# A two-layer transformer block: the second layer's weights split into high and low parts during the first layer and kept in device memory

## The chip, the core and the metric

The kernel runs on one core of a Trainium2 chip. The metric is the device time of one execution in microseconds. TensorE multiplies matrices, VectorE and ScalarE work on rows of 128 partitions, GpSimd (POOL in the rows) does the same more slowly, and SyncE issues the transfers; its queue is called SP in the rows.

## What is computed

A backbone of two layers on 512 latent tokens and 256 context tokens of width 1024. Each layer has a mixing part and a feed-forward part. In short:

```
for l in range(2):
    h  = modulate(rms_norm(x), shift, scale)
    pa, q, k, v, pc = split(h @ w_in[l])       # 2560 columns: A 512, Q 512, K 512, V 512, C 512
    ya = u * (w_s @ layer_norm(v_a))           # group A: gelu, gate mixed over 128 positions
    yb = rms_norm(softmax(q1 k1) v - lam * softmax(q2 k2) v)   # group B: 4 heads, rotary positions
    yc = silu(layer_norm(dwconv31(a * sigmoid(g))))            # group C
    x  = x + gate * (concat(ya, yb, yc) @ w_out[l])
    h2 = modulate(rms_norm(x), ...)
    x  = x + gate2 * ((silu(dwconv3(h2 @ w_gate)) * (h2 @ w_val)) @ w_down)
```

Context tokens go through the same weights. In the second layer only their K and V are needed. The output is the latent stream.

## The kernel before

All matrix products are made three times: every operand is split into a high part (rounded to the type that TensorE takes at full speed, fp32r) and a low part (the rest), and high x high, high x low and low x high are added up in PSUM. So each weight must be split before its use. `wsplit` does that: it loads a tile (512 KB, tag `raw`, three buffers) on the sync queue, makes the high part by a ScalarE copy (line 220) and the low part by a subtraction (line 106) on VectorE or GpSimd, in tiles of tags `hi` and `lo` with two buffers each. Copy and subtraction have a raised priority. Which of the two engines subtracts is written out by hand: `WE` has one letter for each of 20 chunks of w_in and each layer, d for VectorE and p for GpSimd; the calls for w_out, w_gv (gate and value) and w_down name the engine.

One layer runs in stages. In the projection stage, `proj_tok` multiplies the tokens by one block of 512 columns of w_in at a time, in four chunks of 256 rows (`k2`), six or four PSUM tiles of 128 tokens in parallel. For each chunk it first does all products with the high part of the weight (lines 389 and 390), then those with the low part (line 397). The order of the blocks in the second layer is: K for the two context tiles, C (lines 441 to 443), A, K for the four latent tiles, Q, V. Between the products, at fixed steps (`AH`, `KH`, `CH`), hooks put in the small matrix work of the other groups: the gate of A (`pg`), the flips of K into its transposed form (`pk`, line 577), the sums of C's norm (`cm`, `cv`). The depthwise convolution of group C is 60 multiply-adds on VectorE (line 647) with lowered priority, which fill VectorE's gaps; `c_finish` needs all of them. `qk_tile` makes the norm and the rotation of a tile of Q or K on VectorE and ScalarE with two tables GC and GS, which GpSimd makes from ropet and gbase.

Then come the attention stage (scores, softmax, products with V, with a part of the output projection filled in between) and the rest of the output projection (`wout_w`, `wout`). The feed-forward part runs in two halves of 11 blocks of 128 columns: `gv` for each block, then four pairs of output rows (`mp2`) with w_down. In the second half of the first layer the last pair (`tail`) is done first for the context and then for the latent tokens, so that the next layer's norm can begin.

The order on each engine is made when the program is built: a scheduler takes the instructions by priority, which is the order of the code moved by `high_priority` and `low`, and the engines then keep that order. A transfer in the sync queue whose buffer is not yet free therefore holds up all transfers behind it.

## Time and profile before

| | us |
|---|---|
| median of 3 runs (1637.74 to 1638.4) | 1638.32 |
| profiled execution | 1637.72 |
| its span on the chip | 1635.9 |

Busy time in the span: TensorE 1574.7, VectorE 1033.9, ScalarE 646.2, GpSimd 178.3 us. 162.08 MB are moved, at 99 GB/s over the span.

A row of a table of stages gives a stretch, its length, the busy time of each engine in it with the number of instructions, the granted clock of TensorE as a share of full speed, the share of the 16 DMA engines and their GB/s. Groups are instructions with the same line, engine, operation and shape. A busy TensorE need not be at its peak, since products overlap: one product of 512 columns is recorded with some 0.4 us, though the next one starts 0.23 us after it.

### The profile page before, as it was taken

The page shows a single profiled execution, that of the slowest core. Times are in us where ns is not written, and L with a number is a line of the kernel's source. Part 1 is how long each engine was busy: PE and PEld are TensorE (multiplying, and loading weights), DVE is VectorE, ACT ScalarE, POOL GpSimd, SP SyncE. Part 2 cuts the span into 40 slices and gives each one's busy share as a digit, 9 for nine tenths or more (in the row PEclk, how much of TensorE's full clock was granted, in tenths as well). Part 3 has the DMA queues.
Part 4 walks back from the last instruction along what each step waited for, and adds up shares of the span by engine and source line. Part 5 has one row for each costly group of instructions (what it writes and reads, how often), then busy time and mean ns, then how long its engine had stood idle before and what let it go on. Part 6 is the DMA issues. An engine that isn't in the chain of part 4 may idle for free.

```text
span 1635.9 us, 20796 instructions
## 1 busy us (share of the span) xinstructions
PE 1574.7 (96%) x8186; PEld 1294.7 (79%) x8186; DVE 1033.9 (63%) x1666; ACT 646.2 (40%) x1098; POOL 178.3 (11%) x158
## 2 busy tenths in 40 slices
PE   7999998999999999999999999779999999999999
PEld 5865776778888888888888878567778788888888
DVE  4597878969999862244333277996987544244433
ACT  5431568753523221133232244255775433123321
POOL 1130224310000000000000023341420000000000
PEclk8999999999999999999999999889999999999999
DMA  8625110014355852111122223221001223332232
GB/s 286 201 96 171 42 62 14 14 64 169 104 193 194 290 192 70 66 65 62 56 65 58 84 87 110 62 65 52 27 27 65 91 90 96 88 101 97 96 100 94
DMA packets 57409, 162.08 MB, mean 99 GB/s; under 512 B 9056, under 2 KB 11360, under 8 KB 57184
## 3 DMA queue, kind: packets, MB, share of 16 engines
q1 hardware_dynamic: 57312, 160.76, 30.3%
q8 instruction: 64, 1.05, 0.3%
q14 instruction: 33, 0.27, 0.0%
HBM read 158.64 MB, written 2.10 MB: 98 GB/s over the span
## 4 chain that ended last, share of the span: by engine, by line
PE 83%; DVE 10%; ACT 4%; issue 1%; DMA 1%; POOL 0%; POOLq 0%; DVEq 0%; SPq 0%; ACTq 0%
PE pp L227 13%; PE pp L226 13%; PE pp L228 13%; PE pd L228 6%; PE pd L226 6%; PE pd L227 6%; PE acc L389 4%; PE acc L390 4%; PE acc L397 3%; DVE cacc L647 3%; PE po L816 2%; PE mr L156 2%; PE wo L226 1%; PE wo L227 1%; PE wo L228 1%
## 5 line engine op out<-in xcount | busy, mean ns | idle before, releaser
L220 ACT CAST whi<-raw 128x1024 fp32r<-128x1024 f32 (+2 forms) x199 | 204.3, 1029 | 550.9 <-PE pp L227 251.0
L106 DVE TENSOR_TENSOR wlo<-raw,whi 128x1024 fp32r<-128x1024 f32 (+1 forms) x163 | 196.9, 1210 | 304.9 <-ACT whi L220 297.4
L227 PE MATMUL pp<-hlo,whi 128*128 128x512 f32 (+1 forms) x1072 | 380.7, 356 | 0.8 <-DVE hlo L266 0.8
L226 PE MATMUL pp<-hhi,whi 128*128 128x512 f32 (+1 forms) x1072 | 379.8, 356 | 1.5 <-ACT whi L220 1.3
L228 PE MATMUL pp<-hhi,wlo 128*128 128x512 f32 (+1 forms) x1072 | 378.9, 354 | 0.0
L226 PEld LDWEIGHTS pp<-hhi,whi 128*128 128x128 f32 x1072 | 201.4, 188 | 35.1 <-ACT whi L220 2.7
L227 PEld LDWEIGHTS pp<-hlo,whi 128*128 128x128 f32 x1072 | 201.5, 188 | 33.0 <-DVE hlo L266 1.5
L228 PEld LDWEIGHTS pp<-hhi,wlo 128*128 128x128 f32 x1072 | 201.5, 188 | 31.0
L106 POOL TENSOR_TENSOR wlo<-raw,whi 128x1024 fp32r<-128x1024 f32 (+1 forms) x36 | 100.3, 2788 | 870.3 <-ACT whi L220 716.9
L228 PE MATMUL pd<-gh,wlo 128*128 128x512 f32 (+1 forms) x550 | 192.4, 350 | 0.6 <-DVE wlo L106 0.6
L226 PE MATMUL pd<-gh,whi 128*128 128x512 f32 (+1 forms) x550 | 192.9, 351 | 0.0
L227 PE MATMUL pd<-gl,whi 128*128 128x512 f32 (+1 forms) x550 | 192.3, 350 | 0.0
L389 PE MATMUL acc<-whi,hhi 128*128 128x512 f32 x352 | 144.8, 411 | 2.8 <-ACT whi L220 2.8
L390 PE MATMUL acc<-whi,hlo 128*128 128x512 f32 x352 | 144.2, 410 | 0.0
L647 DVE SCALAR_TENSOR_TENSOR cacc<-cin,cw,cacc 128x783 f32<-128x783 f32 (+1 forms) x120 | 125.8, 1102 | 2.8 <-ACT cacc L642 2.7
L228 PEld LDWEIGHTS pd<-gh,wlo 128*128 128x128 f32 x550 | 103.4, 188 | 15.9 <-DVE wlo L106 0.8
L227 PEld LDWEIGHTS pd<-gl,whi 128*128 128x128 f32 x550 | 103.5, 188 | 15.1
L226 PEld LDWEIGHTS pd<-gh,whi 128*128 128x128 f32 x550 | 103.4, 188 | 14.9
L983 DVE TENSOR_TENSOR ft<-ft,pp 128x256 f32<-128x256 f32 (+1 forms) x66 | 39.4, 598 | 96.2 <-PE pp L228 84.7
L397 PE MATMUL acc<-wlo,hhi 128*128 128x512 f32 x352 | 94.0, 401 | 0.0
L389 PEld LDWEIGHTS acc<-whi,hhi 128*128 128x128 f32 x352 | 68.0, 193 | 25.0 <-issue 7.1
L192 DVE CUSTOM_DVE_ANT_0 mraw<-mraw,csil,bmod 128x1024 f32<-128x1024 f32 x64 | 81.7, 1280 | 8.0 <-DMA mraw<-in_w_modT_dram 7.8
(198 smaller groups left out, 2334.3 us busy)
## 6 DMA issues: line engine op xcount, KB each, us to landing
raw<-in_w_gv_dram SPq DMA_DIRECT2D x88, 512.0 KB, 3.2
mraw<-in_w_modT_dram SPq DMA_DIRECT2D x64, 512.0 KB, 4.2
raw<-in_w_in_dram SPq DMA_DIRECT2D x44, 512.0 KB, 3.6
raw<-in_w_down_dram SPq DMA_DIRECT2D x34, 512.0 KB, 3.6
mraw<-in_w_modN_dram SPq DMA_DIRECT2D x16, 512.0 KB, 5.9
mraw<-in_w_modH_dram SPq DMA_DIRECT2D x16, 512.0 KB, 3.9
raw<-in_w_out_dram SPq DMA_DIRECT2D x16, 512.0 KB, 3.2
raw<-in_w_down_dram SPq DMA_DIRECT2D x16, 384.0 KB, 3.2
```

Source lines behind the costliest of these rows:

```text
L106: (eng or V).tensor_sub(o, a, hi.bitcast(F32))
L156: T.matmul(o[r:r + 32], cs[:, k], w, start=k < 4, stop=k >= 4, tile_position=(0, r))
L192: r = V.tensor_tensor_reduce(out=junk, in0=w, in1=csil[:, s], scale=1.0, scalar=bmod[:, l, i, f:f + 1], op0=ALU.mult, op1=ALU.add, accum_o ...
L220: S.copy(hi, raw)
L226: T.matmul(o, lhi, rhi, start=start, stop=False)
L227: T.matmul(o, lhi, rlo, start=False, stop=False)
L228: T.matmul(o, llo, rhi, start=False, stop=stop)
L389: T.matmul(pt[t], hhi[hs], wh[:, a], start=k2 + a == 0, stop=False)
L390: T.matmul(pt[t], hlo[hs], wh[:, a], start=False, stop=False)
L397: T.matmul(pt[t], hhi[hs], wl[:, a], start=False, stop=k2 + 1 == KD // 2 and a == 1)
L647: V.scalar_tensor_tensor(out=cacc[:, c, :cn], in0=cin[:, c, j:j + cn], scalar=cw[:, l, c, j:j + 1], in1=cacc[:, c, :cn], op0=ALU.mult, op1 ...
L983: V.tensor_mul(t[:, a:b], t[:, a:b], pp[s][1][:, :b - a])
```

## The change

The second layer's w_in and w_out are split in the second half of the first layer's feed-forward part (`split_ahead`): 56 pieces of 128x512, each loaded, copied to the high part on ScalarE, subtracted on VectorE, and both parts stored to tiles in device memory. All transfers go by the sync queue. The pieces come at a lowered priority (`ALOW`): up to 3 after each of the 11 blocks of columns and up to 8 after each pair of output rows (`AHEAD`) until there are none left. In the second layer `wsplit_of` loads the two parts (512 KB each) instead of splitting; w_in's odd chunks use two of the three `raw` tiles, the even ones `hi` and `lo`. Two smaller edits concern both layers: GC and GS are made on VectorE, and the low part of w_s is subtracted on VectorE.

```diff
-WE = ("dpdpdpdddppdpppppddp", "pdpppppppppppppddpdd")
+WE = "dpdpdpdddppdpppppddp"
+AHEAD = (3, 8)
+ALOW = 60
...
+    dram = ctx.enter_context(tc.tile_pool(name="split", bufs=1, space=bass.MemoryType.DRAM))
+    split = {}
+
+    def w_cols(l, col, k2):
+        return w_in[l, 2 * k2 * P:(2 * k2 + 2) * P, col:col + 512].rearrange("(a p) n -> p a n", p=P)
+
+    def split_ahead(sp):
+        todo = [(("in", col, k2), [w_cols(1, col, k2)[:, a] for a in range(2)])
+                for col in (COL_K, COL_C, COL_A, COL_Q, COL_V) for k2 in range(KD // 2)]
+        todo += [(("out", q, mp2), [w_out[1, q, mp2, :, i].rearrange("p k m -> p (k m)") for i in range(2)])
+                 for mp2 in range(KD // 2) for q in range(2)]
+        for key, srcs in todo:
+            split[key] = dram.tile([P, 2, 2, 512], F32, name="_".join(map(str, key)))
+            for a, src in enumerate(srcs):
+                raw = sp.tile([P, 512], F32, tag="araw", name="araw", bufs=3)
+                hi = sp.tile([P, 512], F32R, tag="ahi", name="ahi", bufs=3)
+                nc.sync.dma_start(out=raw, in_=src)
+                S.copy(hi, raw)
+                sub_lo(raw, raw, hi)
+                nc.sync.dma_start(out=split[key][:, 0, a], in_=hi.bitcast(F32))
+                nc.sync.dma_start(out=split[key][:, 1, a], in_=raw)
+                yield
+
+    def wsplit_of(key, src, shape, eng, tags=("hi", "lo"), p=None, **kw):
+        if key not in split:
+            return wsplit(src, shape, eng, p=p, **kw)
+        r = []
+        for x, t in enumerate(tags):
+            w = (p or wp).tile([P] + shape, F32R, tag=t, name="w" + "hl"[x], bufs=RAWB if t == "raw" else 2)
+            flat = w.rearrange("p a n -> p a n") if len(shape) == 2 else w.rearrange("p a k m -> p a (k m)")
+            nc.sync.dma_start(out=flat.bitcast(F32), in_=split[key][:, x])
+            r.append(w)
+        return r
...
+            def wchunk(col, k2, **kw):
+                tags = ("raw", "raw") if k2 % 2 else ("hi", "lo")
+                return wsplit_of(("in", col, k2), wsrc(col, k2), [2, 512], wengine(col, k2), tags, **kw)
...
-                    wh, wl = wsplit(wsrc(col, k2), [2, 512], wengine(col, k2))
+                    wh, wl = wchunk(col, k2)
...
-                wh, wl = wsplit(wsrc(COL_C, k2), [2, 512], wengine(COL_C, k2), raw=pre.get(k2))
+                wh, wl = wchunk(COL_C, k2, raw=pre.get(k2))
...
-            wsh, wsl = wsplit(w_sT[l], [HEADS, P], p=sp, **(dict(bufs=1) if l else dict(tags=("mraw", "mraw"), bufs=MRB)))
+            wsh, wsl = wsplit(w_sT[l], [HEADS, P], "dve", p=sp, **(dict(bufs=1) if l else dict(tags=("mraw", "mraw"), bufs=MRB)))
...
-                G.tensor_mul(GC[:, j], ropet[:, 0], gbase[:, j, 0].unsqueeze(1).to_broadcast([P, NLT, QKD]))
-                G.tensor_mul(GS[:, j], ropet[:, 1], gbase[:, j, 1].unsqueeze(1).to_broadcast([P, NLT, QKD]))
+                V.tensor_mul(GC[:, j], ropet[:, 0], gbase[:, j, 0].unsqueeze(1).to_broadcast([P, NLT, QKD]))
+                V.tensor_mul(GS[:, j], ropet[:, 1], gbase[:, j, 1].unsqueeze(1).to_broadcast([P, NLT, QKD]))
...
-            return [(wsplit(w_out[l, q, mp2], [2, 4, P], eng, **kw), (yACh, yACl) if q == 0 else (yBh, yBl))
+            return [(wsplit_of(("out", q, mp2), w_out[l, q, mp2], [2, 4, P], eng, **kw), (yACh, yACl) if q == 0 else (yBh, yBl))
...
+                    if not last and half:
+                        with low(ALOW):
+                            for _ in zip(range(AHEAD[0]), ahead):
+                                pass
...
+                        if not last and half:
+                            with low(ALOW):
+                                for _ in zip(range(AHEAD[1]), ahead):
+                                    pass
...
+                    ahead = split_ahead(wt)
```

## Rows read from the trace of the kernel before

**Rows 1.** The page's busy time: us, share of the span, instructions.

```profile
PE 1574.7 (96%) x8186; PEld 1294.7 (79%) x8186; DVE 1033.9 (63%) x1666; ACT 646.2 (40%) x1098; POOL 178.3 (11%) x158
```

**Rows 2.** Table of stages: stretch, length, busy us (instructions), clock, DMA share, GB/s.

```profile
500.00:600.00 100.00, 100.00 (x568) 87.00 (x567) 91.51 (x160) 28.19 (x34) 0.00 (x0) 1.00 0.76 251
690.00:880.00 190.00, 190.00 (x1079) 165.29 (x1078) 75.33 (x100) 56.15 (x67) 0.00 (x0) 1.00 0.20 64
880.00:945.00 65.00, 65.00 (x374) 56.72 (x373) 20.32 (x29) 14.85 (x21) 2.39 (x1) 1.00 0.26 76
...
1003.50:1107.20 103.70, 81.92 (x363) 64.95 (x361) 99.74 (x142) 44.96 (x81) 38.91 (x17) 0.90 0.25 77
...
1143.50:1232.00 88.50, 82.80 (x433) 66.83 (x431) 75.73 (x139) 66.69 (x152) 30.99 (x45) 1.00 0.07 25
```

**Rows 3.** What TensorE waited for, 940 to 1290 us: total us, times, longest.

```profile
PE pk L577 <- DVE ks L106: 10.9, 3, 4.5
PE pg L226 <- ACT vbh L496: 8.7, 1, 8.7
```

**Rows 4.** Groups by shape, 940 to 1260 us: busy us, mean ns, idle before.

```profile
L647 DVE SCALAR_TENSOR_TENSOR cacc<-cin,cw,cacc 128x512 f32<-128x512 f32 x60 | 62.6, 1095 | 0.8 <-ACT cacc L642 0.8
L106 POOL TENSOR_TENSOR wlo<-raw,whi 128x1024 fp32r<-128x1024 f32 x22 | 57.0, 2590 | 713.1 <-ACT whi L220 643.3 <-PE acc L397 29.7 <-issue 15.3
```

**Rows 5.** The chain that ended last: start us, us, what.

```profile
968.25 0.24 PE acc L389
...
1048.08 0.66 DVE cacc L647
...
1089.09 0.43 PE acc L390
...
1140.61 2.80 PE acc L397 x12
```

**Rows 6.** Order of time, VectorE and GpSimd: start us, us, instructions.

```profile
1007.38 28.34 DVE L647 SCALAR_TENSOR_TENSOR cacc<-cin,cw,cacc 128x512 f32<-128x512 f32 x28 [0.80 <-ACT cacc L642]
...
1073.97 0.16 DVE L557 TENSOR_TENSOR nw<-nw,rk 128x8 f32<-128x8 f32 x1
...
1075.13 3.37 POOL L106 TENSOR_TENSOR wlo<-raw,whi 128x1024 fp32r<-128x1024 f32 x1 [4.66 <-ACT whi L220]
...
1076.15 2.37 DVE L557 TENSOR_TENSOR nw<-nw,rk 128x8 f32<-128x8 f32 x1
```

**Rows 7.** Groups by shape, 940 to 1260 us: a cast and a subtraction of 128x512.

```profile
L106 DVE TENSOR_TENSOR ks<-kx,ks 128x512 fp32r<-128x512 f32 x6 | 4.1, 681 | 1.4 <-ACT ks L595 1.4
...
L595 ACT CAST ks<-kx 128x512 fp32r<-128x512 f32 x6 | 3.7, 620 | 4.8 <-DVE kx L591 4.8
```

**Rows 8.** Transfers: KB each, median us to landing; and GB/s from 410 to 610 us.

```profile
GB/s 3 0 0 113 205 193 124 210 184 215 204 135 210 206 165 196 202 181 170 250 110 210 216 211 288 270 323 310 274 310 324 243 274 243 302 270 217 213 105 79
...
mraw<-in_w_modT_dram SPq DMA_DIRECT2D x53, 512.0 KB, 4.1
...
raw<-in_w_in_dram SPq DMA_DIRECT2D x13, 512.0 KB, 3.6
ropet<-in_rope_dram SPq DMA_DIRECT2D x1, 256.0 KB, 2.6
...
out_dram<-xT SPq DMA_DIRECT2D x4, 256.0 KB, 2.3
```

**Rows 9.** Groups by shape: GC on GpSimd, a product of that size on VectorE.

```profile
L543 POOL TENSOR_TENSOR GC<-ropet,gbase 128x256 f32<-128x256 f32 x2 | 2.4, 1194 | 0.2 <-DVE gbase L541 0.2
...
L565 DVE TENSOR_TENSOR qsq<-kx,GS 128x256 f32<-128x256 f32 x8 | 3.3, 416 | 0.0
```

**Rows 10.** What the sync queue waited for, 960 to 1260 us: total, times, longest.

```profile
SPq L212 <- POOL wlo L106: 134.9, 20, 15.7
...
SPq L536 <- DVE yA L505: 12.3, 1, 12.3
```

More of the change, by code (lines that the diff above doesn't have):

```diff
@@ L314, in wengine @@
             def wengine(col, k2):
-                return {"d": "dve", "p": "pool"}[WE[l][(col - COL_A) // 512 * 4 + k2]]
+                return {"d": "dve", "p": "pool"}[WE[(col - COL_A) // 512 * 4 + k2]]
             def wsrc(col, k2):
-                return w_in[l, 2 * k2 * P:(2 * k2 + 2) * P, col:col + 512].rearrange("(a p) n -> p a n", p=P)
+                return w_cols(l, col, k2)
+            def wchunk(col, k2, **kw):
+                tags = ("raw", "raw") if k2 % 2 else ("hi", "lo")
+                return wsplit_of(("in", col, k2), wsrc(col, k2), [2, 512], wengine(col, k2), tags, **kw)
             if l == 0:
```

## The prediction

> **What bounds the kernel now.** I read the table of stages first, then what TensorE waited for, then the groups of instructions by shape, then the order of time around the longest waits. TensorE is busy for 96% of the span [rows 1], so a change can win only where it is not. The stages [rows 2] show where that is: in the first layer's feed-forward part (500 to 600, 690 to 945 us) it is busy without a gap. In the second layer's projections, 1003.5 to 1107.2 us, it is busy for 81.92 of 103.70 us, at a granted clock of 0.90, while VectorE is busy for 99.74 us. The two long waits of TensorE there are for VectorE's work: 10.9 us on the flips of K (pk) and 8.7 us on group A's gate (pg) [rows 3]. So this stage is VectorE's.
>
> Why is VectorE full there? Its largest group is the depthwise convolution, 60 instructions of 1095 ns [rows 4]. The same instruction takes 0.66 us alone [rows 5], and 28 of them in a row took 28.34 us [rows 6], 1.01 each. What is beside the long ones is GpSimd's subtraction of a weight's low part: 22 of 2590 ns [rows 4]. The plainest case is an operation on 8 columns: 0.16 us alone, 2.37 us when GpSimd's 3.37 us subtraction of 1075.13 us runs [rows 6]. VectorE stands still while GpSimd subtracts. The convolution alone lost 60 x (1.095 - 0.66) = 26 us by it.
>
> **Part 1, the second layer's splits vanish.** Its 24 chunks of w_in and 8 of w_out need no ScalarE cast and no subtraction; 19 + 3 of these subtractions are GpSimd's, those above. First I ask how much TensorE time there is to win. From 968.25 us (its first product for the second layer) to 1143.41 us (the end of V's last) [rows 5] it has 48 + 96 + 96 + 96 + 96 + 144 = 576 products of 512 columns (K of the context, C, A, K, Q, V) at 2.80/12 = 0.233 us [rows 5], 134.4 us; with the flips, the gate and the norms' sums, some 10 us by my estimate, 144. The stretch is 175 us long, so 31 us are idle or run at the low clock: after the waits the same product takes 0.43 us [rows 5], the lower of the two levels, and that passes with the waits.
>
> Then how much VectorE lets it have. Of the 99.74 us in 1003.5 to 1107.2, I take out the convolution's 26 us, the 2.2 us of the operation on 8 columns and one subtraction of 1.2 us, and add 2 us (part 3). 72 us are left. TensorE has C's end at 1003, then A, K, Q with flips and gate, 75 us. So VectorE is no longer the longer of the two, but nearly as long, with chains between them. I give back 23 of the 31 us and leave 8 for waits that remain, or that the longer loads make.
>
> In the attention stage TensorE is idle for 88.50 - 82.80 = 5.7 us [rows 2]; three of GpSimd's subtractions lie there and GpSimd's small operations stay. I take 2 us. Together 25 us.
>
> **Part 2, the splits made in the first layer.** 56 pieces (40 of w_in, 16 of w_out), each a 256 KB load, a cast and a subtraction of 128x512, and two 256 KB stores. They run in the second half of the feed-forward part: 3 after each of 11 column blocks, then 8 after each pair of output rows, 7 in the last. By the nearest rows of that size a cast costs ScalarE 620 ns and a subtraction VectorE 681 ns [rows 7]: 56 x 0.62 = 35 us and 56 x 0.68 = 38 us. From 690 to 945 us these engines are busy for 56.15 + 14.85 = 71 and 75.33 + 20.32 = 96 of 255 us [rows 2]; they come to 106 and 134, and still stand below the 91.51 of 100 us at which VectorE left TensorE without a gap in 500 to 600 us. I cost this at nothing; its cover is TensorE's own work and the two finished weight tiles ahead of it.
>
> The transfers are the closer matter. A column block lasts 48 x 0.233 + 48 x 0.117 = 16.8 us, with 1.05 MB of weights and 3 x 0.79 MB of pieces: 203 GB/s. A pair of output rows lasts 11 x 12 x (0.233 + 0.117)/2 = 23.1 us and carries 1.44 + 8 x 0.79 = 7.7 MB: 335 GB/s. The highest that a slice of the trace shows is 324 GB/s [rows 8], in a stretch whose 512 KB loads took 4.1 us to land and whose products did not wait. So the pieces may fall behind by 7.7/0.324 - 23.1 = 0.7 us for each pair, 2 us in all.
>
> The sync queue is one line: a store there waits for the cast or the subtraction, and a piece's next load waits until one of three buffers has been stored; behind both stand the loads of w_gv and w_down. Those have three raw tiles ahead, about 23 us of TensorE's work, less 6 us for load and split: 17 us of lag cost nothing. One piece is 2.6 (load) + 0.62 + 0.68 + 2.3 (store) = 6.2 us [rows 7, 8]; three at a time give 8 in 16.5 us, within 23.1. Bounds: nothing to a few us; I take 0. A gain is excluded, since TensorE has no gap there.
>
> The Trainium skill, "DMA: Bandwidth & Descriptors", Anatomy of one DMA, says that a transfer's semaphore fires only when the last byte is confirmed in the target memory, and that this can be surprisingly long where the target is HBM. The 256 KB stores at this kernel's end landed in 2.3 us, less than a 256 KB load's 2.6 us [rows 8], so the trace doesn't bear it out for a quiet queue; no run here shows it beside loads. By the row the sum stands; by the page a longer store leads towards rival (c).
>
> **Part 3, small moves.** GC and GS leave GpSimd in both layers: 4 x 1.19 us there in the second layer [rows 9], during which VectorE stalls, become 4 x 0.42 us on VectorE [rows 9]. w_s's low part becomes one subtraction of 0.68 us on VectorE [rows 7]. This is 2 us more for VectorE, counted above. In the first layer the same moves shift an order of work that still has its GpSimd subtractions: from 2 us faster to 2 us slower, I take 0.
>
> **Part 4, the loads of the second layer.** Each chunk is now two 512 KB transfers: 1.05 MB per 5.6 us of products, 187 GB/s, where 324 were seen. The buffers hold 3.5 chunks: a chunk's low part, in a raw tile, is loaded some 11 us before its use, against 3.6 us to land [rows 8]. The K chunks of the context last only 2.8 us each, so there the start hangs on what was fetched during the tail of the first layer: two chunks and a half fit. By my count of the slots the last is due within 1 us of its use. The load of ropet waits 12.3 us in the queue for yA [rows 10], and Q's first chunk is behind it, with one K chunk (5.6 us) of lead for 1.4 MB (4.4 us at 324 GB/s, and some 2 us to land). Bounds: 0 to 8 us; these are the 8 us left standing in part 1. What goes away is the queue's 134.9 us of waiting for GpSimd [rows 10].
>
> **The sum.** 23 + 2 = 25 us. The profiled execution took 1637.72 us (span 1635.9, 1.8 us around it), the median of the three is 1638.32; I hold the two as one. 1638 - 25 = 1613 us.
>
> **Rivals.**
> (a) All of it comes back: 31 + 5.7 us, 1638 - 36 = 1602 us. For it: no row shows another limit. Against it: VectorE's 72 us beside TensorE's 75.
> (b) The double loads become the wait: a chunk's low part late by 1 us in half of the 24 chunks, plus the start and ropet: some 14 us beyond the 8 left standing, 1627 us. For it: the raw tiles' short lead, one queue. Against it: 187 of 324 GB/s.
> (c) The pieces block the sync queue, and the result is slower. Place: the first three pairs of output rows, the 69 us before the last pair. With three buffers a piece may take 23.1 x 3/8 = 8.7 us before any lag, so its stores may take 4.8 us. To undo the 25 us, the lag must reach 17 + 25 = 42 us, 14 for each pair: a piece of 13.9 us, a store of 10 us. If instead the pieces went one at a time, a pair would take 8 x 6.2 = 49.6 us and a column block 18.6: a lag of 3 x 26.5 + 11 x 1.8 = 99 us, less 17, so 82 us lost and 1638 + 82 - 25 = 1695 us. For it: waits of loads and stores in one line. Against it: 2.3 us for a store, and products without a wait at 324 GB/s.
> (d) The change doesn't do what it says: VectorE's long operations have another cause than GpSimd. Then 5 us of subtractions go and 2 come: 1635 us, or no difference. Against it: the 8-column operation of 2.37 us.
>
> **How the numbers follow.** Forecast 0.57, (a) 0.14, (b) 0.15, (c) 0.09 (of that 0.02 with a loss that the gain covers), (d) 0.05. The range reaches from (a) to (b): 1602 to 1628, with the upper part of (c) and (d) left out. A measurement of this kernel can tell about 0.2%, 3.3 us: faster 0.57 + 0.14 + 0.15 + 0.02 = 0.88, and from (d) 0.01; same 0.04; slower 0.07.
>
> **What the changed profile would show.** Step 1: the convolution's instructions at 0.66 to 0.75 us, VectorE no longer full to the end of the stage, the waits pg and pk under 5 us together, the granted clock near 1.0, and the last product of V about 23 us earlier. Step 2: TensorE without idle time from 690 to 945 us, ScalarE and VectorE fuller, and a DMA rate near 300 GB/s in the last 70 us of it. Step 4: waits of products for DMA of whi, wlo below 8 us. I am wrong if TensorE waits for w_gv or w_down weights, if the second layer's products wait for loads in every chunk, or if the convolution stays at 1.1 us with GpSimd quiet.

## The result, and the profile after

The changed kernel takes 1619.74 us, median of four runs (1616.07 to 1622.17), against 1638.24 us for the kernel before on the same chip: a ratio of 0.9886, with a 95% interval of 0.9864 to 0.9908. The profiled execution is the shortest of the four, 1616.07 us (span 1614.0), and stands 21.7 us below that of before. One of four executions of the changed kernel in a later series took 1649.20 us, at the same granted clock as its neighbours; it is not explained, and is left out of everything below.

The page's busy time, beside [rows 1]: VectorE's 1033.9 us became 1020.4, although it has 56 subtractions of pieces more (their casts are ScalarE's), and GpSimd's 178.3 became 105.9.

```profile
PE 1570.6 (97%) x8186; PEld 1292.4 (80%) x8186; DVE 1020.4 (63%) x1722; ACT 646.9 (40%) x1122; POOL 105.9 (7%) x126
```

The table of stages, with the columns of [rows 2] (TensorE, its weight loads, VectorE, ScalarE, GpSimd, clock, DMA share, GB/s). The first two lines are the kernel before: a stretch of the first layer, and the one from TensorE's first product of the second layer to the end of V's last.

```profile
600.00:690.00 90.00, 90.00 (x517) 78.47 (x516) 25.09 (x32) 12.57 (x13) 0.00 (x0) 1.00 0.22 66
...
968.25:1143.41 175.16, 151.33 (x652) 118.99 (x652) 147.97 (x219) 80.30 (x134) 55.02 (x24) 0.93 0.25 75
```

The same view of the kernel after, in the order of time; its stretch from the second layer's first product to V's end is the fourth line, and the fifth is the part of it with A, K and Q, 75 us as the prediction counts TensorE's work there, which was 1003.5 to 1107.2 us before [rows 2].

```profile
600.00:690.00 90.00, 86.74 (x484) 75.09 (x483) 34.53 (x48) 24.05 (x35) 0.00 (x0) 0.98 0.87 284
690.00:880.00 190.00, 185.45 (x1046) 160.88 (x1045) 93.98 (x130) 70.23 (x95) 0.00 (x0) 0.99 0.55 182
880.00:945.00 65.00, 65.00 (x366) 56.55 (x365) 20.73 (x27) 16.23 (x21) 0.00 (x0) 1.00 0.27 82
...
977.80:1121.80 144.00, 144.00 (x652) 115.14 (x651) 107.81 (x219) 56.74 (x110) 1.44 (x1) 1.00 0.55 179
1012.40:1087.40 75.00, 75.00 (x356) 60.78 (x356) 72.84 (x146) 31.18 (x66) 0.00 (x0) 1.00 0.59 189
...
1143.50:1232.00 88.50, 85.38 (x456) 70.26 (x455) 63.15 (x120) 53.14 (x126) 17.04 (x27) 1.00 0.21 72
```

The same 652 products of the second layer's projections took 175.16 us before and 144.00 after, without a gap and at full clock. So 31.2 us came from there. But the stretch begins at 977.80 instead of 968.25: the first layer became 9.6 us longer, and the reader sees where. From 600 to 690 and from 690 to 880 us TensorE is now idle for 90 - 86.74 and 190 - 185.45, together 7.8 us, with a clock below 1; before, it was busy for all 90 us of the former, as its line shows, and for all 190 us of the latter [rows 2]. 31.2 - 9.6 is the 21.7 of the two executions to within 0.1: behind V's end nothing changed (492.5 us to the span's end before, 1614.0 - 1121.8 = 492.2 after).

In the convolution's group from 940 to 1240 us (busy us, mean ns, idle before) one instruction takes 747 ns, where it took 1095 [rows 4]; whether that is why the projections are gapless is tested below.

```profile
L691 DVE SCALAR_TENSOR_TENSOR cacc<-cin,cw,cacc 128x512 f32<-128x512 f32 x60 | 41.6, 747 | 1.4 <-ACT cacc L686 1.4
```

What TensorE waited for in the first layer and at the output projection (total, times, longest). The waits pk and pg of [rows 3] are gone; those for a weight's parts, whi and wlo, are new, since from 590 to 945 us TensorE has no wait at all in the kernel before:

```profile
PE pp L268 <- DVE wlo L110: 4.4, 4, 2.5
...
PE pd L266 <- ACT whi L224: 2.5, 1, 2.5
...
PE wo L266 <- DMA wh<-out: 1.7, 2, 0.9
```

The order of time after, around the longest of these waits, with the first and the last transfer of a piece ahead of and behind it (start, us, what, and in brackets the idle time ahead and what ended it):

```profile
595.67 1.28 SPq L247 DMA_DIRECT2D araw<-in_w_in_dram  x3
...
633.77 6.53 SPq L247 DMA_DIRECT2D araw<-in_w_in_dram  x3
...
640.59 0.62 ACT L248 CAST ahi<-araw 128x512 fp32r<-128x512 f32 x1 [8.71 <-DMA araw<-in_w_in_dram]
641.11 1.04 ACT L224 CAST whi<-raw 128x1024 fp32r<-128x1024 f32 x1
642.20 0.39 PE L266 MATMUL pd<-gh,whi 128*128 128x256 f32 x1 [2.50 <-ACT whi L224]
...
789.16 0.32 SPq L251 DMA_DIRECT2D out<-araw  x1
```

And around the longest wait for wlo:

```profile
700.14 0.69 DVE L110 TENSOR_TENSOR araw<-araw,ahi 128x512 f32<-128x512 f32 x1 [1.91 <-ACT ahi L248]
...
702.85 1.22 DVE L110 TENSOR_TENSOR wlo<-raw,whi 128x1024 fp32r<-128x1024 f32 x1
...
704.12 0.39 PE L268 MATMUL pp<-hhi,wlo 128*128 128x256 f32 x1 [2.46 <-DVE wlo L110]
```

Three things are to be seen. First, the pieces begin at 595.67 us, when the first layer's feed-forward part is still in the w_down of its first half, and are through by 789 us. They don't come three after each block; they come as fast as they are loaded. Second, at 640.59 us ScalarE has stood idle for 8.71 us in front of a piece's cast, because that piece's load hadn't landed; the cast of a weight of w_down comes behind it in ScalarE's order, and TensorE waits for that weight. The granted clock between 640 and 650 us is 0.83. Third, VectorE is such a line too: at 700.14 us it has stood for 1.91 us in front of a piece's subtraction, since the piece's cast was late, and the subtraction of a weight of w_gv comes behind it (after four other operations), with TensorE waiting. No weight's cast is recorded as waiting for its own load from 590 to 850 us.

From 590 to 850 us ScalarE's waits for pieces (total, times, longest):

```profile
ACT ahi L248 <- DMA araw<-in_w_in_dram: 83.7, 28, 8.7
ACT ahi L248 <- DMA araw<-in_w_out_dram: 28.8, 14, 3.7
```

And the transfers of that stretch (count, KB each, median us from issue to landing):

```profile
raw<-in_w_gv_dram SPq DMA_DIRECT2D x22, 512.0 KB, 4.8
araw<-in_w_in_dram SPq DMA_DIRECT2D x40, 256.0 KB, 3.6
in<-ahi SPq DMA_DIRECT2D x40, 256.0 KB, 4.7
in<-araw SPq DMA_DIRECT2D x40, 256.0 KB, 4.9
```

A store of 256 KB took 2.3 us at the quiet end of the kernel before, a load 2.6 [rows 8]; here, where 284 GB/s are moved from 600 to 690 us, it is 4.7 to 4.9 and 3.6 for the pieces of w_in. For those of w_out the same view gives 3.7 to 3.8 for a store and 4.2 for a load.

### The profile page after: what moved, and what is told of

Read it like the earlier page. It is cut to its first block, busy times and chain, and to the rows that moved or that the text cites. A ratio compares the mean times of both kernels' runs of the same rounds, so it can differ in the third digit from the quotient of the medians.

```text
span 1614.0 us, 21207 instructions
## 1 busy us (share of the span) xinstructions
PE 1570.6 (97%) x8186; PEld 1292.4 (80%) x8186; DVE 1020.4 (63%) x1722; ACT 646.9 (40%) x1122; POOL 105.9 (7%) x126
## 2 busy tenths in 40 slices
DMA packets 83140, 222.93 MB, mean 138 GB/s; under 512 B 12256, under 2 KB 14560, under 8 KB 82912
## 3 DMA queue, kind: packets, MB, share of 16 engines
q1 hardware_dynamic: 83040, 221.59, 41.6%
q8 instruction: 64, 1.05, 0.3%
## 4 chain that ended last, share of the span: by engine, by line
PE 77%; DMA 10%; DVE 6%; ACT 4%; issue 2%; SPq 0%; POOL 0%; POOLq 0%; DVEq 0%; ACTq 0%
PE pp L267 10%; PE pp L266 10%; PE pp L268 10%; PE acc L433 5%; PE acc L441 5%; PE acc L434 5%; PE pd L268 4%; PE pd L267 4%; PE pd L266 4%; DMA in<-araw 3%; DMA araw<-in_w_in_dram 3%; PE po L860 3%; PE wo L266 2%; DMA mraw<-in_w_modT_dram 2%; PE wo L267 2%; PE wo L268 2%
## 5 line engine op out<-in xcount | busy, mean ns | idle before, releaser
L224 ACT CAST whi<-raw 128x1024 fp32r<-128x1024 f32 (+1 forms) x167 | 170.9, 1025 | 389.9 <-PE pp L267 203.0
L110 DVE TENSOR_TENSOR wlo<-raw,whi 128x1024 fp32r<-128x1024 f32 (+2 forms) x154 | 185.4, 1206 | 218.4 <-ACT whi L224 211.1
L691 DVE SCALAR_TENSOR_TENSOR cacc<-cin,cw,cacc 128x783 f32<-128x783 f32 (+1 forms) x120 | 103.4, 916 | 3.4 <-ACT cacc L686 3.4
L110 DVE TENSOR_TENSOR araw<-araw,ahi 128x512 f32<-128x512 f32 x56 | 38.5, 691 | 93.3 <-ACT ahi L248 93.2
L248 ACT CAST ahi<-araw 128x512 fp32r<-128x512 f32 x56 | 34.7, 620 | 121.5 <-DMA araw<-in_w_in_dram 83.7
L433 PE MATMUL acc<-whi,hhi 128*128 128x512 f32 x192 | 77.8, 405 | 0.0
L434 PE MATMUL acc<-whi,hlo 128*128 128x512 f32 x192 | 76.9, 401 | 0.0
L101 ACT ACTIVATE ft<-ft 128x768 f32<-128x768 f32 (+1 forms) x44 | 32.6, 740 | 103.2 <-DVE ft L1022 103.2
```

Source lines behind the costliest of these rows:

```text
L110: (eng or V).tensor_sub(o, a, hi.bitcast(F32))
L224: S.copy(hi, raw)
L433: T.matmul(pt[t], hhi[hs], wh[:, a], start=k2 + a == 0, stop=False)
L434: T.matmul(pt[t], hlo[hs], wh[:, a], start=False, stop=False)
L691: V.scalar_tensor_tensor(out=cacc[:, c, :cn], in0=cin[:, c, j:j + cn], scalar=cw[:, l, c, j:j + 1], in1=cacc[:, c, :cn], op0=ALU.mult, op1 ...
```

## The experiments

Two questions were open after this: does GpSimd's subtracting hold VectorE (theory P), and what do the pieces cost and by what? All ratios are against the kernel before on the same chip.

**The changed kernel once more.** No edit. Its four runs had spread over 6 us, and the question was in which part.

> The changed kernel again, nothing edited. Its first profiled execution took 1616.07 us and its four times lie between 1616 and 1622 us, where the kernel before stays within 0.7 us. Theory A (the 56 pieces run as a burst in the sync queue, from about 595 to 790 us, and TensorE waits for weights there, each time a little differently): in this profile the second layer's first product comes some 9 to 14 us after 968.25 us, and the stretch from there to the end of V lasts the same 144 us as in the first profile. Theory B (the spread comes from the second layer's loads): the first layer ends at the same time in both profiles and the 144 us change.

Measured: 1616.62 us, median of three (1615.46 to 1618.81), a ratio of 0.9873 (0.9857 to 0.9890). The high-part products of the projections in this execution (line, shape, durations in ns, first to last):

```profile
L433 PE MATMUL acc<-wh,hhi x160: 392/396/793, 980.9 to 1121.6; 128*128 128x512 f32 x160
```

They last 140.7 us here and, from 977.8 to 1118.5, as long in the first execution. What differs between these two is when they begin, 980.9 against 977.8: theory A. The difference is in the first layer, where the pieces are.

**Two pieces in place of 56.** Only the first tile is split ahead; the other 27 are left out, and all loads of the second layer read the first one instead. The second layer's loads and its work are those of the changed kernel, its weights are not.

```diff
-        for key, srcs in todo:
+        for key, srcs in todo[:1]:
...
-            nc.sync.dma_start(out=flat.bitcast(F32), in_=split[key][:, x])
+            nc.sync.dma_start(out=flat.bitcast(F32), in_=split["in", COL_K, 0][:, x])
```

> Only the first two of the 56 pieces are made, and every load of the second layer reads that one tile in device memory, so the same number of bytes is loaded but the weights of the second layer are not the right ones. Theory A (the pieces cost TensorE some 9 us in the profiled execution, more in the median run): 1607 us, first product of the second layer near 968.5 us, the spread of the runs back under 1 us. Theory B (the loss before the second layer is not the pieces' but comes from the small moves to VectorE or another order of work in the first layer): 1616 to 1620 us, with the first product still at 977 us.

Measured: 1603.48 us (1603.21 to 1604.69), a ratio of 0.9791 (0.9774 to 0.9807).

```profile
L433 PE MATMUL acc<-wh,hhi x160: 389/396/794, 965.0 to 1105.8; 128*128 128x512 f32 x160
```

The projections last 140.8 us as before, but begin at 965.0. So 54 pieces cost 977.8 - 965.0 = 12.8 us in the first execution of the changed kernel and 15.9 in the second; by the medians of this chip it is 1616.62 - 1603.48 = 13.1. That is theory A, with more gained than the 1607 us it named, since 965.0 is also 3.3 us earlier than the 968.25 of before. Whether those 3.3 us are the small moves' is asked below.

**The pieces held back.** The lowered priority didn't pace the pieces. In this version the cast of each piece is put, in the order only, behind the cast that ends the block it follows (or behind the last cast of a weight of w_down).

```diff
-            S.copy(hi, raw)
+            rec[0] = S.copy(hi, raw).ins
...
-                S.copy(hi, raw)
+                r = S.copy(hi, raw)
+                tc.add_manual_dep(r.ins, gate[0].name, NOSYNC, reason="pace")
...
-                    S.copy(gh[:, jj], t[:, :toks])
+                    gate[0] = S.copy(gh[:, jj], t[:, :toks]).ins
...
                         if not last and half:
+                            gate[0] = rec[0]
```

> Each piece's cast is ordered on ScalarE behind the block of the first layer's second half in whose turn it was asked for (the cast of gh, or the last weight cast before it in the output rows). The work and the bytes are the same, only the burst is spread over 690 to 945 us. Theory A1 (the burst is the cost: a rate of 290 GB/s held for 190 us and weights' casts behind pieces' casts that wait for transfers): TensorE without a wait from 600 to 870 us, about 1607 to 1610 us. Theory A2 (56 pieces cost TensorE the same wherever they stand, since the queue is one line): 1616 to 1622 us. With 8 pieces for each pair of output rows at 335 GB/s a few us may come back there: up to 1613 us.

Measured: 1611.63 us (1609.92 to 1614.06), a ratio of 0.9842 (0.9827 to 0.9857). The projections begin at 971.6. The casts of pieces lie between 704.17 and 958.13 us, and up to 945 us TensorE waits for none of them. But one wait is left, at the end, in the order of time:

```profile
946.83 0.62 ACT L250 CAST ahi<-araw 128x512 fp32r<-128x512 f32 x1 [4.83 <-DMA araw<-in_w_out_dram]
...
950.02 0.83 ACT L225 CAST whi<-raw 128x768 fp32r<-128x768 f32 x1
...
950.90 0.58 PE L269 MATMUL pd<-gh,whi 128*128 128x256 f32 x1 [4.07 <-ACT whi L225]
```

It is the picture of 640 us again, with a granted clock of 0.71 between 950 and 960. Eight pieces after a pair of output rows look too many, as their last loads come in when the next weights are due; the version with four tests that.

**GpSimd subtracts again in the second layer.** Of the 20 chunks of w_in, 15 are stored unsplit in the low part's place, and GpSimd subtracts 19 times in the second layer; no cast comes back.

```diff
-                sub_lo(raw, raw, hi)
+                if not on_gp(key):
+                    sub_lo(raw, raw, hi)
...
+        if on_gp(key):
+            with tc.high_priority(offset=400):
+                sub_lo(r[1], r[1].bitcast(F32), r[0], G)
```

> The pieces and the loads stay, but the 15 of 20 chunks of w_in whose low part GpSimd made before are stored unsplit in the low place and GpSimd subtracts again in the second layer (19 subtractions), on tiles that have been loaded; no cast comes back. Theory P (GpSimd's subtractions hold VectorE, and VectorE held TensorE): the convolution's mean goes from 0.75 back to about 1.1 us, the stretch from the second layer's first product to the end of V goes from 144 to some 168 us, and the time to about 1640 us, as slow as before or a little slower. Theory Q (it was the 24 casts and the chain load, cast, subtraction that made TensorE wait): the stretch stays below 150 us and the time below 1625 us.

Measured: 1654.53 us (1651.1 to 1655.01), a ratio of 1.0098 (1.0083 to 1.0113). The stage from its first product to V's end, and the convolution's group:

```profile
983.50:1160.00 176.50, 152.82 (x652) 120.60 (x651) 136.49 (x219) 56.83 (x110) 48.56 (x17) 0.92 0.45 146
```

```profile
L698 DVE SCALAR_TENSOR_TENSOR cacc<-cin,cw,cacc 128x512 f32<-128x512 f32 x60 | 58.5, 1026 | 1.4 <-ACT cacc L693 1.4
```

What TensorE waited for in that stretch:

```profile
PE pg L273 <- ACT vbh L547: 9.2, 1, 9.2
PE pk L628 <- DVE ks L110: 5.5, 2, 3.8
PE pk L628 <- ACT kk L630: 5.0, 1, 5.0
```

When GpSimd subtracts again, the gain in this stretch is gone: 144.0 became 176.5 us, the convolution's instruction 747 became 1026 ns, and pg and pk are back with waits like those of [rows 3]. That is theory P; the time is above the 1640 us it named, as the stretch is 8.5 us longer than its 168 and begins at 983.5, later than the 977.8 and 980.9 of the changed kernel, for a reason that wasn't followed. ScalarE's work is that of the changed kernel (56.83 us), so the casts that the change took away had no part in it. The products waited for GpSimd's own results for only 3.2 us.

**The pieces' cast and subtraction on GpSimd.** This frees ScalarE's order of the pieces and leaves the sync queue's order as it is.

```diff
-                S.copy(hi, raw)
-                sub_lo(raw, raw, hi)
+                G.tensor_copy(hi, raw)
+                sub_lo(raw, raw, hi, G)
```

> Cast and subtraction of the 56 pieces are made by GpSimd, which has nothing else to do in the feed-forward part; transfers, queue and buffers stay. Theory S (TensorE waits because on ScalarE and VectorE, which keep their order, a weight's cast stands behind a piece's cast that waits for its load): TensorE's waits for whi and wlo from 600 to 800 us vanish, the second layer's first product comes near 965 to 968 us instead of 978 to 981, about 1604 to 1607 us. Theory D (it is the sync queue or the rate of the transfers, 290 GB/s): the waits stay, 1613 us or more. VectorE is stalled by GpSimd for up to 56 x 2.6 = 146 us, but is busy for only 96 of 255 us there; if that tells, ft and wlo come late and the time is above 1616 us.

Measured: 1614.4 us (1613.16 to 1615.75), a ratio of 0.9857 (0.9843 to 0.9872); the projections begin at 977.3. By its time that is theory D, but theory S's waits went, as the stages show. The stages where the pieces run:

```profile
600.00:730.00 130.00, 130.00 (x744) 113.31 (x744) 41.41 (x49) 21.85 (x25) 70.06 (x70) 1.00 0.81 264
730.00:800.00 70.00, 61.97 (x329) 51.75 (x328) 22.38 (x30) 16.16 (x20) 36.61 (x39) 0.98 0.83 267
```

And what ScalarE waited for there with its weights' casts:

```profile
ACT whi L224 <- DMA raw<-in_w_gv_dram: 86.3, 14, 9.0
```

The waits at 640 and 704 us are gone, as ScalarE no longer stands in front of a piece; in their place 8 us are lost between 730 and 800 us, where the loads of w_gv come late. They stand in the sync queue behind the pieces' loads and stores, and from 590 to 850 us the stores wait there for GpSimd's results for 88 us in all. The first 130 us ran at 264 GB/s without a gap, so that rate by itself does not hold TensorE. So there are two orders in which a piece can be ahead of a weight, ScalarE's and the queue's. How much of this version's remaining 12 us is the queue and how much is GpSimd holding VectorE stays open.

**The pieces' transfers on GpSimd's queue.** The opposite: the sync queue is free of pieces, ScalarE's order keeps them.

```diff
-                nc.sync.dma_start(out=raw, in_=src)
+                nc.gpsimd.dma_start(out=raw, in_=src)
...
-                nc.sync.dma_start(out=split[key][:, 0, a], in_=hi.bitcast(F32))
-                nc.sync.dma_start(out=split[key][:, 1, a], in_=raw)
+                nc.gpsimd.dma_start(out=split[key][:, 0, a], in_=hi.bitcast(F32))
+                nc.gpsimd.dma_start(out=split[key][:, 1, a], in_=raw)
```

> Only the transfers of the pieces (load and two stores) move from the sync queue to GpSimd's queue; cast and subtraction stay on ScalarE and VectorE. Theory S (the order on ScalarE and VectorE is the cost): no gain, 1614 to 1620 us, with waits for whi and wlo as in the changed kernel. Theory D1 (the pieces' waits in the sync queue delay the weights' loads): waits gone, 1604 to 1608 us. Theory D2 (the rate of the transfers): 1616 to 1622 us and the weights' loads take longer to land than 3.3 us.

Measured: 1976.7 us (1972.98 to 1980.55), a ratio of 1.2069 (1.2050 to 1.2089). The stage, the waits and GpSimd's order of time:

```profile
590.00:850.00 260.00, 109.95 (x498) 90.78 (x496) 40.55 (x59) 27.18 (x39) 43.80 (x80) 0.70 0.30 102
```

```profile
PE pd L266 <- ACT whi L224: 151.3, 9, 20.9
...
PE pp L266 <- ACT whi L224: 72.0, 5, 20.8
...
ACT ahi L248 <- DMA araw<-in_w_in_dram: 230.0, 27, 22.6
```

```profile
643.33 0.54 POOL L251 DMA_DIRECT2D in<-araw  x1 [2.40 <-issue]
...
646.28 0.54 POOL L250 DMA_DIRECT2D in<-ahi  x1 [2.41 <-issue]
```

None of the three theories had this. GpSimd issues one transfer in some 2.95 us, so a piece with its three takes 9 us; ScalarE stands in front of each (230.0 us from 590 to 850 us), and TensorE behind ScalarE for 223 us from 400 to 1000 us. Only 102 GB/s are moved. So the order on ScalarE by itself, at a low rate, can cost TensorE that much; how the changed kernel's 12.8 to 15.9 us divide, this run can't say. The Trainium skill, "DMA: Bandwidth & Descriptors", Issuing engines are not separate DMA queues, calls the time that a sequencer needs to initiate a transfer usually small beside the transfer. In this trace it wasn't small for GpSimd: 2.95 us from one issue to the next, against 2.7 to 2.9 us from issue to landing for the same transfers.

**Held back, four at a time.** The version that holds the pieces back, with one more number changed.

```diff
-AHEAD = (3, 8)
+AHEAD = (4, 4)
```

> As e3_paced, but 4 pieces in each block of columns (250 GB/s by my count) and 4 in each pair of output rows (199 GB/s) instead of 3 and 8 (203 and 335). In e3_paced the one long wait, 4.1 us and a low clock after it, stood in the output rows near 948 us. If the crowding of pieces there is what remained of the cost: 1604 to 1607 us and the first product of the second layer near 966 us. If the cost goes with the number of pieces alone: 1610 to 1613 us as in e3_paced.

Measured: 1603.17 us (1601.04 to 1604.36), a ratio of 0.9787 (0.9773 to 0.9802). The stage with all pieces (their casts lie between 704.86 and 941.67 us), and the projections:

```profile
680.00:950.00 270.00, 269.51 (x1552) 235.33 (x1551) 136.64 (x193) 102.69 (x147) 0.00 (x0) 1.00 0.71 229
```

```profile
L436 PE MATMUL acc<-wh,hhi x160: 392/396/794, 966.3 to 1107.0; 128*128 128x512 f32 x160
```

The same 56 pieces, the same transfers and the same three buffers now cost 966.3 - 965.0 = 1.3 us. This kernel is level with the one that makes two pieces, and 13.5 to 16.6 us faster than the two medians of the changed kernel.

**No split ahead; VectorE subtracts.** The kernel before, with all subtractions of the second layer's w_in and w_out given to VectorE. If GpSimd's sharing is what cost, this alone should bring most of the gain.

```diff
-WE = ("dpdpdpdddppdpppppddp", "pdpppppppppppppddpdd")
+WE = ("dpdpdpdddppdpppppddp", "dddddddddddddddddddd")
...
-                    wout(mp2, (0,), wout_w(mp2, (0,), "pool"), whole, ps, "f", FB)
+                    wout(mp2, (0,), wout_w(mp2, (0,), "dve" if l else "pool"), whole, ps, "f", FB)
```

> The kernel before, with all subtractions of the second layer (19 of w_in, 3 of w_out) on VectorE instead of GpSimd; nothing is made ahead, all casts and chains stay. Theory P (GpSimd stalls VectorE for nearly its whole subtraction): in the projections VectorE gets 13 x 1.22 us more work and loses some 13 x 2 us of stalls, the convolution's mean falls to about 0.75 us, the time to 1622 to 1632 us. Theory Q (the chains load, cast, subtraction hold TensorE): no gain or slower, 1636 to 1645 us, since VectorE has more to do.

Measured: 1622.05 us (1620.4 to 1624.41), a ratio of 0.9900 (0.9884 to 0.9917). A stage in the projections and the one at the start of attention:

```profile
1050.00:1100.00 50.00, 49.34 (x242) 39.88 (x241) 49.90 (x100) 28.42 (x55) 4.00 (x4) 1.00 0.26 78
...
1115.00:1160.00 45.00, 35.10 (x149) 27.04 (x148) 39.25 (x83) 25.18 (x60) 10.04 (x19) 0.81 0.07 24
```

```profile
L647 DVE SCALAR_TENSOR_TENSOR cacc<-cin,cw,cacc 128x512 f32<-128x512 f32 x60 | 42.5, 760 | 0.8 <-ACT cacc L642 0.8
```

VectorE makes more subtractions than before, and the projections still come down from 175 to 145 us (969.2 to 1114.3), with the convolution at 760 ns. TensorE has hardly a gap from 1050 to 1100 us although VectorE is full (49.90 of 50). But VectorE's last convolution instruction starts at 1099.8 us, where it was 1087.0 in the changed kernel, and the last steps of C and the norm of Q come after V's end, where attention waits for some of them:

```profile
PE pss L769 <- DVE qlz L106: 3.3, 1, 3.3
```

From V's end to the end of its span, 1622.6 us, there are 508.3 us, 16 more than before.

**The small moves alone.** The kernel before with GC, GS and w_s's low part on VectorE.

```diff
-                G.tensor_mul(GC[:, j], ropet[:, 0], gbase[:, j, 0].unsqueeze(1).to_broadcast([P, NLT, QKD]))
-                G.tensor_mul(GS[:, j], ropet[:, 1], gbase[:, j, 1].unsqueeze(1).to_broadcast([P, NLT, QKD]))
+                V.tensor_mul(GC[:, j], ropet[:, 0], gbase[:, j, 0].unsqueeze(1).to_broadcast([P, NLT, QKD]))
+                V.tensor_mul(GS[:, j], ropet[:, 1], gbase[:, j, 1].unsqueeze(1).to_broadcast([P, NLT, QKD]))
```

> The kernel before with the two small moves alone: GC, GS and the low part of w_s are made on VectorE in both layers. The two-piece run reached the second layer 3.2 us before the kernel before did, and 2.2 us of that stood already at the start of the first feed-forward part. Theory M (these 3 us are the small moves'): 1634 to 1636 us, first layer's feed-forward part 2 us earlier; in the second layer, where GpSimd still subtracts, another 0 to 2 us. Theory N (they come from the second layer's chunks no longer being split at the end of the first): 1637 to 1639 us, no change.

Measured: 1634.3 us (1633.26 to 1635.49, ten runs) against 1638.51, a ratio of 0.9977 (0.9967 to 0.9987): 4.2 us, as theory M has it. The first layer's feed-forward products begin at 404.0 us, 2.4 earlier than the 406.4 of before; in all profiled executions with the moves they begin between 402.4 and 405.0, in the one other without them at 408.3. The second layer begins at 965.7, also 2.4 us earlier than the 968.1 of before.

**Both without pieces.** The last two edits together.

> The kernel before with the second layer's subtractions on VectorE (e8) and the two small moves (e9) together, nothing made ahead. If the parts add up: e8's 1622 less 2 to 4 us, 1618 to 1620 us, level with the changed kernel, so that the pieces and their cost bring nothing over it, while the paced pieces (1603 us) bring 16 us over it. If GC and GS on VectorE delay K's chain, which is VectorE's in this kernel: 1622 us or more.

Measured: 1620.25 us (1619.97 to 1621.28), a ratio of 0.9894 (0.9879 to 0.9908).

```profile
1115.00:1160.00 45.00, 35.24 (x160) 28.04 (x158) 40.11 (x81) 24.73 (x59) 8.06 (x16) 0.85 0.07 24
```

The start of attention is as it was with the first edit alone, 35.24 of 45 us busy. This kernel splits nothing ahead, moves no more bytes than before (162.08 MB, against 222.93 in the changed kernel), and can't be told from the changed kernel by its time. Taking GpSimd's subtractions away is what gains; making the splits earlier gives back in attention what the pieces, as the change orders them, take in the feed-forward part.

## Why the prediction was nearly right, and where two terms cancel

The forecast was 1613 us with a range of 1602 to 1628. The median came out 7 us higher, the profiled execution 3 us higher. Faster was right, and so was the reason given for it. But the terms were wrong on both sides.

**What bounds the kernel: right.** VectorE stood still while GpSimd subtracted. Putting GpSimd's subtractions back, and nothing else, brought the whole stretch back (176.5 us), and taking them away without any split ahead took it away (145 us). Rival (d) is out. The forecast of the convolution, 0.66 to 0.75 us, held at 0.747, but its lower end was a misreading. The 0.66 us of [rows 5] is the step from one instruction to the next on the chain; the recorded time of that same instruction, which overlaps the next, is 0.74:

```profile
1048.01 0.74 DVE L647 SCALAR_TENSOR_TENSOR cacc<-cin,cw,cacc 128x512 f32<-128x512 f32 x1
```

A mean of 1.095 has to be set beside 0.74, and the convolution lost 60 x (1.095 - 0.74) = 21 us and not 26: its busy time went from 62.6 to 41.6. What made up for it is that two groups of K's norm and rotation, kx<-kx,rk and kx<-kx,GC, had been stretched as well (1047 and 1144 ns before, 688 after, 4 us together), which I hadn't counted. So VectorE's 72 us beside TensorE's 75 came out at 72.84 of 75.00, by two errors that nearly cancel.

**Part 1, the give-back: too small.** The 31 us there to win were counted rightly: the work of 144 us worked out from the products is to the microsecond what the stretch now takes. I gave back 23 and held 8 for waits that remain, since VectorE's 72 us seemed hardly shorter than TensorE's 75. All came back, as rival (a) has it for this stretch: from 1012.4 to 1087.4 us VectorE is busy for 72.84 of 75.00 us and leaves TensorE no gap. The step that failed is that I took nearness to full for a loss, a quarter of the gain. A row against it was in my own hands: VectorE busy for 91.51 of 100 us beside a TensorE without a gap [rows 2]. I used it to price the pieces and not here.

**Part 4, the double loads: right that they could do, wrong to keep a price.** Q's chunk behind ropet and the short lead of the low parts were held at 0 to 8 us. The stretch has no gap at 179 GB/s, so they cost nothing there; at the output projection TensorE waits 1.7 us for wh. Rival (b) is out as well.

**Attention: 2 us forecast, 0.3 measured.** The stage's idle time reads 3.1 us after 5.7, but that window now holds work that came 22 us later before; from V's end to the span's end the kernel got 0.3 us shorter. Of TensorE's waits from 1120 to 1300 us, 0.8 us for GpSimd's subtraction are gone and those 1.7 us for wh are new.

**Part 2, the pieces: this step failed.** I took 0, with bounds of "nothing to a few us"; they cost 12.8 to 15.9. Two of its statements were false. The first is "3 after each of 11 column blocks, then 8 after each pair": that is the order of the code, and I read a lowered priority as a time. From 595 us on all 56 pieces ran as a burst, and from 880 to 945 us only 82 GB/s were moved, where I had forecast near 300. The second is "the cover is the two finished weight tiles": I counted how much work the engines had, 106 and 134 of 255 us, and not what stands behind a piece. A cast that waits for its load holds all casts behind it, and the next weight's is one of them; the same holds for VectorE's subtractions. I had asked that question of the sync queue and not of ScalarE and VectorE. TensorE waiting for weights of w_gv and w_down was my own sign of being wrong, and it came. Held behind the blocks and taken four at a time, the same pieces cost 1.3 us, so the busy shares had been right and the order was the fault. Holding them back also lowered the rate, from 284 GB/s (600 to 690 us) to 229 (680 to 950); how much of a late load in the burst was due to the rate, and how much to the three buffers, stays open.

**The price of a store.** I took 2.3 us; it was 4.7 to 4.9 for the pieces of w_in and 3.7 to 3.8 for those of w_out. The prediction had set the sentence on write receipts beside its row, the Trainium skill, "DMA: Bandwidth & Descriptors", Anatomy of one DMA, that a transfer's semaphore waits until the last byte is confirmed, surprisingly long where the target is HBM. That section is on transfers issued by GpSimd, and these go by the sync queue. The trace doesn't separate a receipt from plain crowding: a 256 KB load, which targets SBUF, got longer too, from 2.6 to 3.6 us for w_in, and for w_out the loads (4.2) took longer than the stores. By these medians a piece of w_in became 3.6 + 0.62 + 0.68 + 4.8 = 9.7 us, above the 8.7 that rival (c) allowed. What happened is a relative of that rival, at a small part of its price, and on ScalarE and VectorE; a weight's own load that came late and held TensorE was seen only with the pieces' casts on GpSimd.

**Part 3, the small moves: 0 forecast, 4.2 us measured.** They gained 4.2 us by themselves, 2.4 of it ahead of the second layer's first product, where my bounds were 2 us on either side. The version with two pieces begins that layer another 0.7 us earlier (965.0 against 965.7), which is not shown to be theirs. The first layer has the same GpSimd instructions in front of the same VectorE work, and I should have priced it like the second; which of the moved operations gained it wasn't tested.

**The sum.** 31 + 0.3 + 3.3 - 12.8 = 21.8, against 21.7 between the two executions; the last two terms are both taken from the version with two pieces, so that the sum closes says nothing on how they divide. Mine was 23 + 2 + 0 - 0 = 25. I held 8 us too little for the projections, gave attention 2 that it didn't yield, missed 3 ahead of the second layer and missed 13 of the pieces; that the total came out within 7 us is partly luck.

## What to carry to other kernels

When VectorE is full beside a busy GpSimd, look first at the duration of one VectorE instruction with and without GpSimd beside it, both read from the same kind of row: moving GpSimd's work to the full engine may be most of the gain, by a change of two lines. An engine that is nearly full is no loss by itself; look for the wait behind it. Work that is done ahead of its time has to be put in order behind something that paces it, since the lowered priority held nothing back here. For each step that is moved, ask on every in-order line that it enters, engine or queue, what stands right behind it, and price it by that and not by the busy share.

## What the runs showed of the hardware

A load of a piece that lands late costs more than its wait, as the clock falls beside it: TensorE was busy for 9.70 of 10 us at a granted clock of 1.00 from 630 us on, then for 7.04 of 10 at 0.83, with the wait of 2.50 us. From 950 to 960 us of the version with the pieces held back it is 0.71, behind the wait of 4.07.

Where GpSimd subtracted in the second layer's projections (17 times there), one convolution instruction on VectorE took 1026 ns on average, without it 747; an operation on 8 columns took 2.37 us in place of 0.16 [rows 6].

Transfers issued by GpSimd came 2.95 us apart for 256 KB each, 0.54 of it the instruction itself; on the sync queue the issue of one is 0.32 us.

The second layer's projections ran without a gap while each chunk of 5.6 us loaded 1.05 MB, at 179 GB/s, all on one queue.
